# A hybrid decoder trunk on one core: norms spread by transposes, some norm sums from one operand, and first products, an attention turn and the last tile reordered

## The chip, the cores and the metric

The kernel runs on one core of a Trainium2 chip. The metric is the device time of one execution in microseconds. A kernel's time is the median of its runs; the profile is one further execution, with the time of every instruction on TensorE (matrix products into PSUM), VectorE, ScalarE, GpSimd and SyncE (which issues the DMAs).

## The reference, cut to what matters

Two residual layers over 1024 tokens of width 1024, all in float32, with a norm ahead of every mixer and feed-forward part and one at the end. Layer 0 mixes with gated DeltaNet heads and a short convolution, layer 1 with HGRN2 heads and dilated window attention in three patterns that are merged by their log-sum-exp.

```python
def rms_norm(x, g):
    xf = x.astype(jnp.float32)
    y = xf * lax.rsqrt(jnp.mean(xf * xf, axis=-1, keepdims=True) + EPS)
    return (y * g.astype(jnp.float32)).astype(x.dtype)
...
    for layer in range(DEPTH):
        i = layer // 2
        hn = rms_norm(h, norm_mix_g[layer])
        if layer % 2 == 0:
            h = h + mixer_ab(...)
        else:
            h = h + mixer_cd(...)
        hn = rms_norm(h, norm_ffn_g[layer])
        h = h + swiglu(hn, ffn_w_gate[layer], ffn_w_up[layer], ffn_w_down[layer])
    return rms_norm(h, norm_final_g)
...
    o_a = gated_delta_rule(q, k, v, g, beta)
    o_a = (rms_norm(o_a, norm_g) * jax.nn.silu(z...)).reshape(b, t, DN_VW)
...
    wts = jax.nn.softmax(jnp.stack(lses, axis=-1), axis=-1)
    o_d = jnp.einsum('bthpd,bthp->bthd', jnp.stack(outs, axis=3), wts)
```

## The kernel before, in words

Activations lie transposed: 128 features on the partitions, 512 tokens (a "half") along a row, eight such pieces a half. Every projection is a sum over eight pieces of three products each (`mm3`, lines 122 to 128): a float32 operand is split into a rounded high part and a rest (`split`: ScalarE makes the high part, VectorE the rest), and high x high, high x rest and rest x high are added in PSUM. So a projection of one 128-feature tile for one half is 24 products of 512 columns (`proj`). Weights come in tiles of 512 KB through two `raw` buffers, and are split into four `w` buffers (`wload`). PSUM has eight banks in three kinds: `psg` (2), `psu` (3), `psm` (3); a product that asks for a bank waits until the last reader of that bank's earlier tile is done.

The norms are made by the class `Trunk`. `piece` squares one of the eight pieces on ScalarE and adds it to `acc` (on GpSimd unless told otherwise), but keeps the last square apart (L183 to L187). `rms` (L189) sums over the features with one-column products against a column of 1/1024: four token blocks for `acc`, four for the last square (L199); a product of plain float32 operands runs as two instructions. VectorE adds EPS (L202) and GpSimd takes the power -0.5 (L204). `spread` (L208) brings the four columns of factors to a row on all partitions with four plain products of a broadcast column against the identity (L213). ScalarE and VectorE then scale.

The order of the work. Where `manual_schedule` names an engine, that engine's instructions run in the order in which they are written; elsewhere a planner orders them by costs and due times. Each engine's queue is run in order, SyncE's too. The places that matter here:

- The start (L2355 to L2397): by hand on TensorE, VectorE and ScalarE. The first four weight tiles are `w0` and `w1` twice (`coming` asks, `arrived` splits a whole tile); `scaled_in` makes the two parts of one piece of x, `squares` the squares with adds on VectorE. `mixer_ab` (L1140 to L1155) then makes three products of the first half, with the norm's sum and spread between, then a fourth, then two products of the second half around the second norm (`second(0)` to `second(3)`). `lead` takes such a product out of its bank on VectorE (L1137).
- `gated` (L1587 to L1608), once for each of eight chunks of the DeltaNet: a diagonal matrix is made of the norm factors on VectorE (L1600), and four plain products of head rows with it transpose and scale in one (L1603).
- `Up.turn` (L583 to L700), by hand: the start of each feed-forward part, and through `Pairs` of the layer-1 projections. `part_a` splits a weight; `early` holds for `Pairs`. `rms(1, between=low)` puts VectorE's small step (L202) where it is written.
- `mixer_cd`: value products, query and key products (`swa_qk`, which frees its bank at L1963), HGRN2 steps and attention steps are interleaved by `tick` and `run`. `turns` rotates the queries and keys of pattern 0 (three VectorE operations each, L1917 to L1919); `run` advances it with every second HGRN2 step. `combine` (L2141) merges three patterns' parts of one head and half: it loads the parts that lie in DRAM (L2149), waits one or two steps, computes on VectorE (L2157 to L2174) and transposes into a `psu` bank (L2181).
- `out_proj` (L1092): asks for the eight pieces of h of a half (`tr.begin`, L167) and then for the weights, pair by pair (L115); `save` writes h back (L217).
- `down` and, for its very last tile, `last` (L1014): the tile's 512 tokens as two halves of 256 columns with TensorE's order by hand, each followed by its norm, the scaling of all eight pieces (`scaled`, L2411) and the writing out.

Of the kernel before, what the change touches and what calls it, by code (L numbers as in the profile page):

```python
# [54 lines left out]
def hybrid_trunk_kernel(ctx: ExitStack, tc: tile.TileContext, x_t, w_all, w_down, w_ba, vecs, c_f, c_i, c_rope, out):  # L55
# [92 lines left out]
    class Trunk:  # L148
# [23 lines left out]
        def piece(self, half, d, eng=None, cols=ALL, n=None):  # L172
# [11 lines left out]
            if n == KT - 1:  # L184
                self.sq[half] = q
            else:
                (eng or G).tensor_tensor(a, a, q, op=ADD)  # L187

        def rms(self, half, cols=ALL, between=lambda: None):  # L189

            a = self.acc[half][:, cols]
            q = self.sq.pop(half)
# [4 lines left out]
            for i, x in enumerate((a, q)):  # L197
                for j in range(n):
                    T.matmul(st[:, j:j + 1], x[:, j * P:(j + 1) * P], onesn, start=i + j == 0, stop=i == 1,  # L199
                             skip_group_check=True)  # L200
# [7 lines left out]
        def spread(self, r):  # L208
# [3 lines left out]
            for j in range(n):  # L212
                T.matmul(pb[:, j * P:(j + 1) * P], r[:, j:j + 1].to_broadcast([P, P]), ident, start=True, stop=True)  # L213
# [39 lines left out]
    class Up:  # L253
# [335 lines left out]
        def turn(self, tr, row, b11, b21, hx, close, left, right):  # L589
# [21 lines left out]
            self.part_a(1, ga)  # L611
            self.part_a(2, w2)
# [5 lines left out]
            dg = tr.rms(1, between=low)  # L618
            self.p2(0, b21, psg())
# [364 lines left out]
    def down(layer, up, tr, hx, hr, src, step, after):  # L984
# [29 lines left out]
        def last(part, d):  # L1014

            a, b = slice(0, HT // 2), slice(HT // 2, HT)
            with tc.manual_schedule(engines={mybir.EngineType.PE}):
                oa, ob = psu(), psm()
                part(oa, range(NK), a)
                add(1, d, oa, a)  # L1020
                part(ob, range(3), b)
                r = tr.rms(1, a)
                part(ob, range(3, 7), b)
                scaled(1, a, tr.spread(r))
                part(ob, range(7, NK), b)
                add(1, d, ob, b)
                scaled(1, b, tr.spread(tr.rms(1, b)))
# [64 lines left out]
    def out_proj(name, cat_d, tr, src, order, half, hp, lead=None):  # L1092
# [18 lines left out]
    def mixer_ab(hn, rb, hp, tr, first, second, close):  # L1111
# [46 lines left out]
        with ExitStack() as es:  # L1158
# [305 lines left out]
            def delta(yd, xd, load_al, load_cx):  # L1464
# [123 lines left out]
                def gated(c):  # L1588
# [10 lines left out]
                    dg = bt("dgo", bufs=1)  # L1599
                    V.tensor_tensor(dg, ident[:, None, :].to_broadcast([P, 4, P]), hb(rr), op=MULT)  # L1600
# [55 lines left out]
    def mixer_cd(hn, hp, pairs):  # L1656
# [7 lines left out]
        with ExitStack() as es:  # L1664
# [320 lines left out]
            class Attend:  # L1985
# [114 lines left out]
                def outputs(self, n):  # L2100
# [8 lines left out]
                    if n % 2 == 0:  # L2109
                        return  # L2110
# [444 lines left out]
```

## Time and profile before

| what | us |
|---|---|
| three runs | 2591.68, 2594.03, 2596.03 |
| their median | 2594.03 |
| the profiled execution, whole | 2596.2 |
| its span, first to last instruction | 2594.4 |
| TensorE busy | 2557.3 |
| VectorE busy | 1666.6 |
| ScalarE busy | 1034.5 |
| GpSimd busy | 515.9 |

A row of the timeline is: start, duration, engine, line, operation, out<-in, shape, how many; in brackets the engine's idle time before it and what ended it. PE is TensorE's products, PEld its weight loads, DVE VectorE, ACT ScalarE, POOL GpSimd, SPq SyncE's issues. Matrix products are pipelined, so the time that one costs is from its start to the next one's start, not its duration. The mean clock granted to TensorE was 0.996 of full.

### The profile page before, as it was taken

The numbers are of one execution on the slowest core, as the hardware profiler recorded it, in microseconds if no ns is written. First come the engines' busy times: TensorE is split into PE (matmuls) and PEld (weight loads), VectorE is DVE, ScalarE is ACT, GpSimd is POOL, SyncE is SP. The second block draws the span as 40 slices with busy tenths as digits, with TensorE's granted clock in tenths as the row PEclk, the third lists the DMA queues.
The fourth block names the chain that finished last, engine by engine and source line by source line (L and its number), as shares of the span: only waits on it lengthen the run. The fifth ranks groups of instructions, "written<-read, shape, count | busy, mean of one in ns | idle before, by whom it ended". The sixth has DMA issues, their size and how long they took to land. (4 is left out here: it accounts for less than half of the span.)

```text
span 2594.4 us, 37707 instructions
## 1 busy us (share of the span) xinstructions
PE 2557.3 (99%) x14179; PEld 2131.5 (82%) x14179; DVE 1666.6 (64%) x2814; ACT 1034.5 (40%) x1855; POOL 515.9 (20%) x440
## 2 busy tenths in 40 slices
PE   8999999999999999999999999999999999999998
PEld 6888888888888888888888887888788888888887
DVE  7877776576655665557675576674667565566553
ACT  4432123343333345344344455564534333334442
POOL 1111021344333310023330000000023433331001
PEclk9999999999999999999999999999999999999999
DMA  4334446525556688643336676525652455668853
GB/s 143 124 113 135 136 132 204 182 66 174 171 196 209 203 288 300 188 132 130 118 114 229 200 225 212 147 87 179 212 195 73 171 177 195 203 210 281 280 177 119
DMA packets 286375, 456.03 MB, mean 176 GB/s; under 512 B 50128, under 2 KB 141040, under 8 KB 286064
## 3 DMA queue, kind: packets, MB, share of 16 engines
q1 hardware_dynamic: 286192, 453.62, 53.9%
q8 instruction: 111, 1.82, 0.3%
q14 instruction: 72, 0.59, 0.1%
HBM read 311.36 MB, written 142.16 MB: 175 GB/s over the span
## 5 line engine op out<-in xcount | busy, mean ns | idle before, releaser
L103 DVE TENSOR_TENSOR w<-raw,w 128x1024 fp32r<-128x1024 f32 (+1 forms) x319 | 384.1, 1207 | 134.7 <-ACT w L102 133.5
L102 ACT CAST w<-raw 128x1024 fp32r<-128x1024 f32 (+1 forms) x319 | 306.6, 963 | 274.1 <-PE psu L128 127.3
L126 PE MATMUL psu<-hnh,w 128*128 128x512 f32 x888 | 355.9, 401 | 10.5 <-ACT w L102 8.8
L128 PE MATMUL psu<-hnh,w 128*128 128x512 f32 x888 | 349.4, 394 | 0.2
L127 PE MATMUL psu<-hnl,w 128*128 128x512 f32 x888 | 348.5, 392 | 0.8 <-DVE hnl L2339 0.8
L126 PEld LDWEIGHTS psu<-hnh,w 128*128 128x128 f32 x888 | 168.3, 190 | 45.0 <-ACT w L102 8.9
L128 PEld LDWEIGHTS psu<-hnh,w 128*128 128x128 f32 x888 | 168.0, 189 | 36.9 <-DVE w L103 1.3
L127 PEld LDWEIGHTS psu<-hnl,w 128*128 128x128 f32 x888 | 168.3, 190 | 34.8 <-DVE hnl L2339 1.3
L187 POOL TENSOR_TENSOR acc<-acc,sq 128x512 f32<-128x512 f32 x48 | 70.5, 1469 | 524.5 <-ACT sq L183 410.6
L302 POOL TENSOR_TENSOR ws<-raw 128x512 f32<-128x512 f32 x50 | 72.8, 1455 | 424.4 <-DMA raw<-in_dram 330.5
L103 DVE TENSOR_TENSOR w<-ws,w 128x1024 fp32r<-128x1024 f32 x47 | 61.7, 1313 | 118.2 <-ACT w L102 118.2
L103 DVE TENSOR_TENSOR hidq<-hr,hidq 128x1024 fp32r<-128x1024 f32 x72 | 82.1, 1142 | 77.1 <-ACT hidq L102 76.9
L102 ACT CAST hidq<-hr 128x1024 fp32r<-128x1024 f32 x72 | 70.2, 979 | 103.2 <-DMA hr<-ts 59.5
L126 PE MATMUL psm<-hidq,w 128*128 128x512 f32 (+1 forms) x275 | 106.0, 385 | 0.0
L127 PE MATMUL psm<-hidq,w 128*128 128x512 f32 (+1 forms) x275 | 105.8, 385 | 0.0
L128 PE MATMUL psm<-hidq,w 128*128 128x512 f32 (+1 forms) x275 | 105.8, 385 | 0.0
L126 PE MATMUL psu<-t3h,w 128*128 128x512 f32 x224 | 87.3, 390 | 1.0 <-ACT u L365 1.0
L126 PE MATMUL psu<-t4h,w 128*128 128x512 f32 x224 | 87.5, 391 | 0.6 <-ACT c L372 0.5
L127 PE MATMUL psu<-t4l,w 128*128 128x512 f32 x224 | 87.2, 389 | 0.0
L127 PE MATMUL psu<-t3l,w 128*128 128x512 f32 x224 | 87.1, 389 | 0.0
L128 PE MATMUL psu<-t4h,w 128*128 128x512 f32 x224 | 87.1, 389 | 0.0
L128 PE MATMUL psu<-t3h,w 128*128 128x512 f32 x224 | 87.1, 389 | 0.0
(491 smaller groups left out, 6479.2 us busy)
## 6 DMA issues: line engine op xcount, KB each, us to landing
raw<-in_dram SPq DMA_DIRECT2D x227, 512.0 KB, 4.4
sd<-in_dram SPq DMA_DIRECT2D x44, 512.0 KB, 3.9
hid<-hid SPq DMA_DIRECT2D x88, 256.0 KB, 3.1
sd<-sd SPq DMA_DIRECT2D x44, 512.0 KB, 3.4
hr<-ts SPq DMA_DIRECT2D x40, 512.0 KB, 4.2
raw<-sd SPq DMA_DIRECT2D x40, 512.0 KB, 4.4
hd<-h SPq DMA_DIRECT2D x48, 256.0 KB, 3.8
h<-hd SPq DMA_DIRECT2D x48, 256.0 KB, 5.4
```

The lines of the kernel that those rows point to most:

```text
L102: S.copy(hi, src)
L103: eng.tensor_tensor(lo, src, hi.bitcast(F32), op=SUB)
L126: T.matmul(o, lh, rh, start=first and i == 0, stop=False, **kw)
L127: T.matmul(o, lh, rl, start=False, stop=False, **kw)
L128: T.matmul(o, ll, rh, start=False, stop=last and i == n - 1, **kw)
L187: (eng or G).tensor_tensor(a, a, q, op=ADD)
L302: G.tensor_tensor(s[:, HT:], b[:, :HT], b[:, HT:], op=ADD)
```

## The change

The norm: the last square is added like the others, except in second halves with GpSimd's adds; the sum takes one operand where there is one; the spread is four transposes.

```diff
             q = self.tmp("sq", bufs=2)[:, cols]
             S.activation(q, src, AF.Square)
-            if n == KT - 1:
+            if n == KT - 1 and half and eng is None:
                 self.sq[half] = q
...
-            q = self.sq.pop(half)
+            parts = [a, self.sq.pop(half)] if half in self.sq else [a]
...
-                T.matmul(pb[:, j * P:(j + 1) * P], r[:, j:j + 1].to_broadcast([P, P]), ident, start=True, stop=True)
+                T.transpose(pb[:, j * P:(j + 1) * P], r[:, j:j + 1].to_broadcast([P, P]), ident)
```

The mixer rows of layer 0 are scaled on VectorE and then transposed:

```diff
-                    V.tensor_tensor(dg, ident[:, None, :].to_broadcast([P, 4, P]), hb(rr), op=MULT)
+                    V.tensor_tensor(rows, os_all[c], hb(rr), op=MULT)
...
-                        T.matmul(o[:, h * P:(h + 1) * P], os_all[c][:, h, :], dg[:, h, :], start=True, stop=True)
+                        T.transpose(o[:, h * P:(h + 1) * P], rows[:, h, :], ident)
```

The start: sixteen products of constants into a bank that nothing reads; the first two weights split by halves, between the pieces of x; the first products by halves of their sum, and three of the second half ahead of the last `second`:

```diff
+    o = psg()
+    for _ in range(16):
+        T.matmul(o[:, 0:P], onesn.to_broadcast([P, P]), onesn.to_broadcast([P, P]), start=True, stop=True)
...
     scaled_in(0, 0)
-    first = [[arrived(*w0)], []]
+    first = [[w0[0], w1[0]], []]
+    for i in range(2):
+        arrived_half(i, *w0)
     for d in range(1, 4):
         scaled_in(0, d)
-    first[0].append(arrived(*w1))
+    for i in range(2):
+        arrived_half(i, *w1)
+        for d in range(4 + 2 * i, 6 + 2 * i):
+            scaled_in(0, d)
...
-        os3 = [proj(wk(wqk, 0), hn[0]), proj(wk(wqk, 1), hn[0])]
+        a, b = range(KH), range(KH, KT)
+        os3 = [proj(wk(wqk, i), hn[0], a, last=False) for i in range(2)]
+        for i in range(2):
+            proj(wk(wqk, i), hn[0], b, os3[i], first=False)
+        os3.append(proj(wk(wvz, 0), hn[0], a, last=False))
         r = tr.rms(0)
-        os3.append(proj(wk(wvz, 0), hn[0], range(KH), last=False))
+        proj(wk(wvz, 0), hn[0], b, os3[2], first=False)
+        o = proj(wk(wvz, 1), hn[0], a, psg(), last=False)
         pb = tr.spread(r)
-        proj(wk(wvz, 0), hn[0], range(KH, KT), os3[2], first=False)
+        early[0, 3] = proj(wk(wvz, 1), hn[0], b, o, first=False)
         second(0)
...
-        early[0, 3] = proj(wk(wvz, 1), hn[0])
         second(1)
         early[1, 0] = proj(wk(wqk, 0), hn[1])
+        early[1, 1] = proj(wk(wqk, 1), hn[1])
         second(2)
-        early[1, 1] = proj(wk(wqk, 1), hn[1])
+        early[1, 2] = proj(wk(wvz, 0), hn[1])
         second(3)
```

The turn of `Pairs`: two weight splits after the norm's small step.

```diff
             if not self.early:
                 self.part_a(0, g0)
-            self.part_a(1, ga)
-            self.part_a(2, w2)
+                self.part_a(1, ga)
+                self.part_a(2, w2)
...
             dg = tr.rms(1, between=low)
+            if self.early:
+                self.part_a(1, ga)
+                self.part_a(2, w2)
```

The output projection asks for h two pieces at a time:

```diff
-        tr.begin(half, src)
+        tr.begin(half, src, range(2))
         for d0 in range(0, KT, 2):
             w = ws.get(d0) or wload((name, d0), (name, d0 + 1))
+            if d0 + 2 < KT:
+                tr.load(half, src, range(d0 + 2, d0 + 4))
```

Layer 1's mixer: no rotation is advanced while query and key products are being made; the merge of a part that has just been computed asks for the two others one attention step earlier (`partners`, in the tile that the rotations used before, or in the old ones), and computes one step after its own part is there:

```diff
-                        if begun[0] % 2:
+                        if begun[0] % 2 and made[0] <= len(coming):
                             next(turner, None)
...
                     if n % 2 == 0:
+                        if self.p == 0 and (self.h, 1, 1) in ended:
+                            self.others = partners(self.h, n // 2)
                         return
...
-                    if p == 0 and (h, 1, 1) in ended:
-                        late.append(combine(h, g, (ol, sums)))
-                        next(late[-1])
+                    if self.others:
+                        late.append(combine(h, g, (ol, sums, *self.others)))
+                        self.others = None
                         return
...
                 yield
-                if unit or ahead:
+                if not own and (unit or ahead):
                     yield
```

The last tile: 256, 128 and 128 columns, by hand on VectorE and ScalarE too, each norm's spread later among the next part's products:

```diff
-            a, b = slice(0, HT // 2), slice(HT // 2, HT)
-            with tc.manual_schedule(engines={mybir.EngineType.PE}):
-                oa, ob = psu(), psm()
+            a, b, c = slice(0, HT // 2), slice(HT // 2, 3 * HT // 4), slice(3 * HT // 4, HT)
+            E = mybir.EngineType
+            with tc.manual_schedule(engines={E.PE, E.DVE, E.Activation}):
+                oa, ob, oc = (psu() for _ in range(3))
                 part(oa, range(NK), a)
                 add(1, d, oa, a)
-                part(ob, range(3), b)
-                r = tr.rms(1, a)
-                part(ob, range(3, 7), b)
-                scaled(1, a, tr.spread(r))
-                part(ob, range(7, NK), b)
+                part(ob, range(5), b)
+                ra = tr.rms(1, a)
+                part(ob, range(5, NK), b)
                 add(1, d, ob, b)
-                scaled(1, b, tr.spread(tr.rms(1, b)))
+                pa = tr.spread(ra)
+                scaled(1, a, pa)
+                part(oc, range(3), c)
+                rb = tr.rms(1, b)
+                part(oc, range(3, NK), c)
+                add(1, d, oc, c)
+                pb = tr.spread(rb)
+                rc = tr.rms(1, c)
+                scaled(1, b, pb)
+                scaled(1, c, tr.spread(rc))
```

More of the change, by code (lines that the diff above doesn't have):

```diff
@@ L196, in rms @@
             st = psm()
-            for i, x in enumerate((a, q)):
+            for i, x in enumerate(parts):
                 for j in range(n):
-                    T.matmul(st[:, j:j + 1], x[:, j * P:(j + 1) * P], onesn, start=i + j == 0, stop=i == 1,
-                             skip_group_check=True)
+                    T.matmul(st[:, j:j + 1], x[:, j * P:(j + 1) * P], onesn, start=i + j == 0,
+                             stop=i == len(parts) - 1, skip_group_check=True)
             v = self.tmp("v4", (4,), 2)[:, 0:n]
@@ L2139, in outputs, with outputs_of, partners @@
                         late.extend(combine(h, i) for i in range(2))
+            def outputs_of(h, g, p, a):
+                dma(a[:, :, 0:P + 2],
+                    scr_o[h, p, g * HT:(g + 1) * HT].rearrange("(j i) d -> i j d", i=P)[:, :, 0:P + 2])
+            def partners(h, g):
+                if g:
+                    both = tl("turn0", (2, 4, 132))
+                    ts = [both[:, p] for p in range(2)]
+                else:
+                    ts = [tl(f"cm{p}", (4, 132)) for p in range(2)]
+                for p, a in enumerate(ts):
+                    outputs_of(h, g, p, a)
+                return ts
             def combine(h, g, own=None):
@@ L2145, in combine @@
                         yield
-                t, st = ([own[0]], [own[1]]) if own else ([], [])
-                for p in range(2) if own else (2, 0, 1):
-                    a = tl(f"cm{p}", (4, 132))
-                    dma(a[:, :, 0:P + 2],
-                        scr_o[h, p, g * HT:(g + 1) * HT].rearrange("(j i) d -> i j d", i=P)[:, :, 0:P + 2])
-                    t.append(a)
-                    st.append(a[:, :, P:P + 2])
+                if own:
+                    t, st = [own[0], *own[2:]], [own[1]]
+                else:
+                    t, st = [tl("cm2", (4, 132))] + [tl(f"cm{p}", (4, 132)) for p in range(2)], []
+                    for p, a in zip((2, 0, 1), t):
+                        outputs_of(h, g, p, a)
+                st += [a[:, :, P:P + 2] for a in t[len(st):]]
                 yield
-                if unit or ahead:
+                if not own and (unit or ahead):
                     yield
@@ L2374, in hybrid_trunk_kernel, with arrived_half @@
     dma(cf[:, 0:P], c_f[:, 0:P])
+    o = psg()
+    for _ in range(16):
+        T.matmul(o[:, 0:P], onesn.to_broadcast([P, P]), onesn.to_broadcast([P, P]), start=True, stop=True)
+    def arrived_half(i, u, raw):
+        z = slice(i * HT, i * HT + HT)
+        split(u[:, 0, z], u[:, 1, z], raw[:, z])
     scaled_in(0, 0)
-    first = [[arrived(*w0)], []]
+    first = [[w0[0], w1[0]], []]
+    for i in range(2):
+        arrived_half(i, *w0)
     for d in range(1, 4):
         scaled_in(0, d)
-    first[0].append(arrived(*w1))
+    for i in range(2):
+        arrived_half(i, *w1)
+        for d in range(4 + 2 * i, 6 + 2 * i):
+            scaled_in(0, d)
     w0, w1 = coming(("ab", 8)), coming(("ab", 12))
@@ L2384, in hybrid_trunk_kernel @@
     dma(ci, c_i)
-    for d in range(4, KT):
-        scaled_in(0, d)
     squares(0, range(3))
```

6 lines of the change are left out of this document (3 added, 3 removed).

## The prediction

> **What bounds the kernel now.** I read the page first, then TensorE's waits, longest first, then the timeline around each of them.
>
> ```profile
> span 2594.4 us, 37707 instructions
> PE 2557.3 (99%) x14179; PEld 2131.5 (82%) x14179; DVE 1666.6 (64%) x2814; ACT 1034.5 (40%) x1855; POOL 515.9 (20%) x440
> ```
>
> The span is TensorE's: 99% busy. An edit can gain in three ways only: fewer or cheaper TensorE instructions, TensorE waits that go, and a clock that is not granted in full. The waits are few (us in all, times, longest):
>
> ```profile
> PE psu L126 <- ACT w L102: 8.8, 2, 6.9
> PE psu L126 <- DVE k L1963: 4.1, 1, 4.1
> PE psm L213 <- POOL r L204: 3.3, 2, 2.2
> PE psu L2181 <- DVE ol L2174: 2.1, 2, 1.6
> ```
>
> Of the first row 6.9 us is the start, so the other wait for a weight is 1.9. The clock is the third item. In the timeline (start, duration) a 512-column product follows its predecessor after 0.23 us, and after 0.42 us inside a stretch with half the clock. The table of windows (us, busy by engine, clock, DMA) shows such stretches, 3.41 us or twice that long:
>
> ```profile
> 24.54 0.40 PE L126 MATMUL psu<-hnh,w 128*128 128x512 f32 x1
> 24.77 0.39 PE L127 MATMUL psu<-hnl,w 128*128 128x512 f32 x1
> ...
> 26.19 0.63 PE L128 MATMUL psu<-hnh,w 128*128 128x512 f32 x1
> 26.61 0.63 PE L126 MATMUL psu<-hnh,w 128*128 128x512 f32 x1
> ```
>
> ```profile
> 25.09:28.50 3.41, 3.41 (x11) 2.76 (x10) 1.65 (x3) 0.00 (x0) 0.54 (x1) 0.50 0.25 97
> 1598.64:1602.05 3.41, 3.24 (x9) 2.59 (x10) 0.02 (x1) 0.00 (x0) 0.00 (x0) 0.50 0.98 309
> 1899.00:1905.83 6.83, 6.83 (x22) 5.67 (x22) 3.15 (x5) 2.82 (x3) 1.97 (x1) 0.50 0.79 246
> ```
>
> A stretch of 3.41 us at half clock costs 3.41 x (1 - 0.23/0.42) = 1.5 us. Each follows a wait or a run of one-column products.
>
> **The change part by part.** First the TensorE instructions (start of a block, then of what follows it; by line for the counts):
>
> ```profile
> 49.99 1.05 PE L213 MATMUL psm<-cf,r 128*128 128x128 f32 x8
> 50.80 0.48 PE L1183 MATMUL psu<-hnh,wba 128*16 128x512 f32 x1
> ```
>
> ```profile
> 1836.69 0.60 PE L2181 MATMUL psu<-cf,ol 128*128 128x128 f32 x4
> 1837.04 0.48 PE L126 MATMUL psu<-b22h,w 128*128 128x512 f32 x1
> ```
>
> ```profile
> 2557.89 1.03 PE L199 MATMUL psm<-onesn,sq 128*128 128x1 f32 x8
> 2558.78 0.49 PE L126 MATMUL psg<-hidq,w 128*128 128x512 f32 x1
> ```
>
> ```profile
> L213 PE MATMUL psm<-cf,r 128*128 128x128 f32 x80 | 11.2, 282 | 3.3 <-POOL r L204 3.3
> L1603 PE MATMUL psm<-dgo,os 128*128 128x128 f32 x64 | 8.5, 276 | 0.1
> ```
>
> Four plain products run as eight instructions, 0.81 us; four transposes of the same size as four, 0.35 us: 0.46 less. Spreads: x80 is nine whole ones and two half ones, 9 x 0.46 = 4.1 us (the halves are in the last tile, below). Mixer rows: x64 is eight chunks, 8 x 0.46 = 3.7 us; the VectorE multiply ahead of them keeps its size. Sums: the second operand's eight instructions take 0.89 us, and six norms lose them (first half of five, and the first mixer's second half): 5.3 us. Together 13.1 us. In their place one more add runs ahead of each of the six sums, on GpSimd or VectorE; more products lie between for all but the first and the one near 1896, where up to its length can be given back. [...]
>
> The start:
>
> ```profile
> 10.46 1.05 ACT L102 CAST w<-raw 128x1024 fp32r<-128x1024 f32 x1 [0.54 <-DMA raw<-in_dram]
> 20.40 1.48 DVE L187 TENSOR_TENSOR acc<-acc,sq 128x512 f32<-128x512 f32 x2
> 21.94 1.05 PE L199 MATMUL psm<-onesn,acc 128*128 128x1 f32 x8 [0.17 <-DVE acc L187]
> 52.41 1.28 DVE L1137 TENSOR_TENSOR xp<-psu,rb 128x512 f32<-128x512 f32 x2
> ```
>
> ```profile
> 30.00:60.00 30.00, 30.00 (x145) 21.96 (x143) 28.70 (x48) 13.54 (x22) 5.60 (x10) 1.00 0.14 45
> ```
>
> The 16 dummy products run while TensorE waits for data anyway; their 32 instructions, at 0.10 us or twice that at half clock, end between 4 and 7.5, when the first weight is there (6.9 before), so I cost them at nothing. The second weight lands at 10.4; its first half is cast by about 11.1, and 36 of the first 48 products then follow at 0.23: done near 19.5 instead of 21.9. With 12 more (22.2) the sum waits for VectorE, whose chain ended at 21.9 and now has another 0.74: 22.6. The low stretch there (0.17 idle and sixteen one-column instructions, 1.9 us) shrinks to 1.2, so I take the half-clock stretch at 25.09 as gone. Then three products for the second half are made ahead of the second spread, instead of two. They hold all three banks of their kind, and no other product can start until VectorE has read one (52.41 before; it is busy 28.70 of 30 us around it). By my count TensorE comes to that point at 49.7 and waits to about 52.1, with 24 products (5.5 us) more behind it than at 50.80 before: 4.1 us ahead, 2.7 of which are already counted (two spreads, two sums). That leaves 1.4. VectorE, so full here, will make TensorE wait for some of this later in the mixer: I take 1.0 back (bounds 0 and all 4.1). Net 0.4.
>
> The turn at 1164:
>
> ```profile
> 1163.39 1.22 DVE L103 TENSOR_TENSOR w<-raw,w 128x1024 fp32r<-128x1024 f32 x1
> 1166.74 1.16 PE L213 MATMUL psm<-cf,r 128*128 128x128 f32 x8 [2.21 <-POOL r L204]
> 1167.94 2.72 DVE L223 SCALAR_TENSOR_TENSOR h<-h,vec,psm 128x512 f32<-128x512 f32 x4 [2.13 <-PE psm L213]
> 1190.64 0.50 PE L128 MATMUL psg<-t1h,w 128*128 128x512 f32 x1 [0.48 <-DVE w L289]
> ```
>
> The norm's small VectorE step stands behind two weight splits of 1.22 us; they now come after it. The spread need not wait, but VectorE then has those splits ahead of its scaling, and sets the pace up to 1190: 1167.94 becomes about 1165.9. 2.0 us (bounds 1.0 and 2.4).
>
> The rotations in the attention products:
>
> ```profile
> 1592.35 0.69 DVE L1917 TENSOR_TENSOR rs<-rs,turn 128x512 f32<-128x512 f32 x1
> 1597.63 1.03 DVE L1963 TENSOR_TENSOR k<-psu,sw 128x512 f32<-128x512 f32 x1
> ```
>
> TensorE waits 4.1 us for the bank that L1963 frees. Behind it on VectorE stand the three operations of a rotation, 0.69 each; held back, they give 2.1 us and run under the next value products. Bounds: 0, and 4.1 with 1.5 for the half-clock stretch behind it. Value 2.1.
>
> Merging the attention parts, and the loads of the output projection:
>
> ```profile
> 1857.53 0.17 DVE L2158 TENSOR_TENSOR mx<-mx,cm 128x4 f32<-128x4 f32 x1 [1.93 <-DMA cm<-scr_o]
> ...
> 1886.20 2.44 SPq L167 DMA_DIRECT2D h<-hd  x5
> 1891.31 0.92 SPq L115 DMA_DIRECT2D raw<-in_dram  x2
> 1897.22 1.04 ACT L102 CAST w<-raw 128x1024 fp32r<-128x1024 f32 x1 [5.58 <-DMA raw<-in_dram]
> ```
>
> The parts are asked for one step of the attention earlier, so VectorE's waits for them go; with them TensorE's 2.1 us of L2181. The merge itself now starts a step later where nothing follows. The tiles that only change shape cost nothing: the rotations that used the shared one are done before. Value 2.0, bounds -1 and 3.5. In the projection eight loads of h stand in SP's queue and on the DMA engines ahead of the weight for which TensorE stops 1.9 us; now two do, the others follow weights. With that wait the two half-clock stretches go: 1.9 + 2 x 1.5 = 5.0 us (bounds 0 and 5.5). The later h loads have over 10 us to land.
>
> The last tile:
>
> ```profile
> 2577.32 0.28 PE L126 MATMUL psu<-hidq,w 128*128 128x256 f32 x1
> 2578.76 0.28 PE L126 MATMUL psm<-hidq,w 128*128 128x256 f32 x1
> ...
> 2584.05 0.50 PE L199 MATMUL psm<-onesn,acc 128*128 128x1 f32 x4
> 2588.12 2.42 DVE L2411 TENSOR_TENSOR h<-h,psm 128x1024 f32<-128x1024 f32 x3 [1.65 <-PE psm L213]
> ```
>
> Twelve products of 256 columns take 1.44 us, 0.12 each. Two quarters of 128 columns are 66 products in place of 33. No such product is in the trace. Nearest are the 128-column passes at 0.10 to 0.11, so 66 x 0.11 = 7.3 us in place of 4.0: 3.3 more. The other end is two passes for each, as a plain product of this width has: 0.22, another 7.3. Behind the last product stand 10.3 us now. A quarter needs about 1.5 us of scaling instead of 2.42, but with VectorE's order by hand the second quarter's 1.5 stands ahead of it: about 8.7. Net 1.7 us lost (bounds 0 and 9.0).
>
> **The sum.** 13.1 + 0.4 + 2.0 + 2.1 + 2.0 + 5.0 - 1.7 = 22.9 us. The profiled execution took 2596.2 us, 1.8 around its span; it becomes 2573.3. The median shown is 2594.0, 2.2 lower, so 2571.
>
> **The rivals.**
> - *Queues as before.* The loads and rotations are ordered by a planner outside the hand-written stretches; the weight at 1891.31 may stand behind a save of h as much as behind the loads (SP is in order), and the bank at 1594 may wait for another VectorE split. Then 2.1 + 2.0 + 5.0 = 9.1 us stay: 2580. For it: neither queue is written by hand there. Against it: six loads fewer stand in front.
> - *Two passes in the last tile.* 128-column products at 0.22: 2578. For it: plain products of this width have two passes. Against it: one instruction a product at 256 and 512.
> - *More goes than I count.* The clock stays full after 1594 as well, the banks come sooner, the last tile breaks even: about 2561.
> - *VectorE takes the cut.* TensorE's shorter blocks turn into waits for VectorE in the mixers, and the queues stay: 13.1 + 0.4 + 9.1 lost, 2594. Against it: outside the first 110 us VectorE has slack (64%).
> - *The clock gate shuts at the transposes* (slower). If they do not keep the clock up, each of the nine spreads and eight chunks costs a half-clock stretch: 17 x 1.5 = 26 us, 2597. [...] The transposes at 1836.69 stand outside every half-clock stretch, so the trace does not bear it out at this length.
>
> **How the numbers follow.** Forecast 2571 (2564 to 2577): 0.55. Queues as before 0.15, two passes 0.15, more goes 0.08, VectorE takes the cut 0.05, the gate shuts 0.02. The range 2561 to 2583 takes in the third rival's time and the first two's, with part of what lies beyond each, and leaves out the last two. This kernel's measurement can tell about 0.2% (5 us) from no change: faster 0.55 + 0.15 + 0.15 + 0.08 = 0.93, same 0.05, slower 0.02.
>
> **What would show it.** L213's and L1603's successors with blocks of 0.35 us; six sums of eight instructions; TensorE at full clock from about 6 us on and through 25 to 28; a wait of some 2 us at the first product after the second spread; no wait at the turn's spread; L1963's wait halved; no TensorE stop at the weight near 1896, and the clock full there; the last tile's 128-column step. I am wrong if the bank wait near 50 is over 5 us, if TensorE's waits between 60 and 110 grow by more than 2, or if that step is near 0.2.

## The result, and the profile after

| | before | after |
|---|---|---|
| median, us | 2594.31 (6 runs, 2591.68 to 2599.68) | 2574.34 (6 runs, 2570.22 to 2577.98) |
| profiled execution, whole | 2596.2 | 2570.22 |
| its span | 2594.4 | 2568.4 |

The ratio is 0.9922, 95% interval 0.9910 to 0.9934: 20.0 us less between the medians, where 22.9 were forecast, and 26.0 between the two profiled spans. The median lies inside the forecast's range of 2564 to 2577, 3.3 us above its 2571. The profiled execution of the changed kernel is the fastest of its six runs, that of the kernel before stands 1.9 us above its median; what makes one execution differ from the next is read further down.

From the page of the changed kernel (busy time, share and instructions by engine):

```profile
PE 2544.8 (99%) x14124; PEld 2120.3 (83%) x14124; DVE 1666.6 (65%) x2823; ACT 1034.8 (40%) x1859; POOL 522.6 (20%) x445
```

TensorE's busy time fell by 12.5 us, with 33 products added in the last tile and 32 instructions at the start. Its waits by what ended them (us in all, times, longest):

```profile
PE psu L126 <- ACT sw L1909: 2.4, 1, 2.4
PE psu L126 <- DVE k L1981: 2.1, 1, 2.1
...
PE psm L213 <- POOL r L204: 1.5, 2, 1.0
...
PE psm L199 <- POOL acc L187: 0.9, 1, 0.9
```

L1981 is the old L1963: 4.1 became 2.1. The waits for the merge (old L2181) and for the weight near 1896 are not in the list; a wait of a sum for GpSimd is new. The timeline has the new blocks, and the place where I expected a wait for a bank:

```profile
28.97 0.60 PE L213 MATMUL psm<-cf,r 128*128 128x128 f32 x4
29.33 0.48 PE L126 MATMUL psg<-hnh,w 128*128 128x512 f32 x1
...
43.04 0.95 PE L199 MATMUL psm<-onesn,acc 128*128 128x1 f32 x8
43.85 0.49 PE L126 MATMUL psu<-hnh,w 128*128 128x512 f32 x1
...
49.87 1.89 PE L1371 MATMUL psg<-kq 128*128 128x256 f32 x8
52.03 0.41 PE L1201 MATMUL psu<-hnh,wba 128*16 128x512 f32 x1 [0.27 <-DVE xp L1150]
...
338.87 0.60 PE L1621 MATMUL psm<-cf,dgo 128*128 128x128 f32 x4
339.23 0.48 PE L126 MATMUL psu<-hnh,w 128*128 128x512 f32 x1
```

From block to next start: spread 0.36 us, sum 0.81, mixer rows 0.36, as forecast. Where all three `psu` banks are held, the planner had put eight products into a `psg` bank (L1371), so TensorE stood still for only 0.27 us.

The table of windows (us, busy by engine, clock, DMA share, GB/s): full clock around 25 and 1899, and one half-clock stretch left ahead of TensorE's last product, behind the first wait of the list.

```profile
22.40:30.00 7.60, 7.53 (x39) 6.40 (x40) 3.12 (x8) 2.19 (x5) 1.47 (x1) 1.00 0.51 167
...
1840.00:1900.00 60.00, 58.95 (x266) 47.82 (x265) 33.84 (x42) 25.55 (x34) 14.23 (x10) 1.00 0.82 276
```

```profile
1546.64:1550.05 3.41, 1.34 (x11) 1.15 (x11) 2.41 (x8) 3.31 (x10) 0.00 (x0) 1.00 0.44 138
1550.05:1553.46 3.41, 3.12 (x7) 2.48 (x8) 1.88 (x5) 2.97 (x8) 0.00 (x0) 0.50 0.72 238
```

Where the 26.0 us came from is told by the lead: how much earlier the same piece of TensorE's work starts (a spread L213, a chunk's transposes, or the n-th product of lines 126 to 128).

| place (start before, after) | lead, us | gained since, of it cheaper instructions |
|---|---|---|
| first chunk's rows (345.04, 338.87) | 6.2 | 6.2, 2.7 |
| first feed-forward, second spread (529.16, 517.42) | 11.7 | 5.6, 5.0 |
| turn's spread (1166.74, 1151.89) | 14.9 | 3.1, 1.8 |
| end of the turn, product 4620 (1189.5, 1175.8) | 13.8 | -1.1, 0.5 |
| product 6720 (1720.0, 1703.6) | 16.4 | 2.6, 0 |
| behind the merge, product 7140 (1873.7, 1852.9) | 20.8 | 4.4, 0 |
| spread in the output projection (1918.95, 1892.89) | 26.1 | 5.3, 0.9 |
| last tile's first product (2574.81, 2547.88) | 26.9 | 0.9, 2.3 |
| end | 26.0 | -0.9, 0 |

### The profile page after: what moved, and what is told of

It is laid out like the page before. It is cut to its first block, busy times and chain, and to the rows that moved or that the text cites. A ratio compares the mean times of both kernels' runs of the same rounds, so it can differ in the third digit from the quotient of the medians.

```text
span 2568.4 us, 37628 instructions
## 1 busy us (share of the span) xinstructions
PE 2544.8 (99%) x14124; PEld 2120.3 (83%) x14124; DVE 1666.6 (65%) x2823; ACT 1034.8 (40%) x1859; POOL 522.6 (20%) x445
## 4 chain that ended last, share of the span: by engine, by line
PE 73%; DVE 6%; DMA 2%; ACT 1%; issue 1%; POOL 0%; SPq 0%; DVEq 0%; ACTq 0%; POOLq 0%
PE psu L126 13%; PE psu L128 13%; PE psu L127 13%; PE psg L126 5%; PE psg L128 5%; PE psg L127 5%; PE psm L128 4%; PE psm L127 4%; PE psm L126 4%; PE psm L2125 1%; DVE h L223 1%; DVE h L592 1%; PE psm L2067 1%; DMA raw<-in_dram 1%; DVE w L289 1%
## 5 line engine op out<-in xcount | busy, mean ns | idle before, releaser
L126 PE MATMUL psu<-hnh,w 128*128 128x512 f32 x880 | 350.9, 399 | 2.8 <-ACT sw L1909 2.4
L128 PE MATMUL psu<-hnh,w 128*128 128x512 f32 x880 | 345.1, 392 | 1.0 <-DVE w L103 1.0
L187 POOL TENSOR_TENSOR acc<-acc,sq 128x512 f32<-128x512 f32 x52 | 79.0, 1520 | 527.1 <-ACT sq L183 527.0
L126 PE MATMUL psm<-hidq,w 128*128 128x512 f32 x264 | 102.8, 389 | 0.0
L127 PE MATMUL psm<-hidq,w 128*128 128x512 f32 x264 | 102.8, 389 | 0.0
L128 PE MATMUL psm<-hidq,w 128*128 128x512 f32 x264 | 102.8, 389 | 0.0
L126 PE MATMUL psu<-hidq,w 128*128 128x512 f32 (+2 forms) x242 | 90.7, 375 | 0.0
L127 PE MATMUL psu<-hidq,w 128*128 128x512 f32 (+2 forms) x242 | 90.5, 374 | 0.0
L128 PE MATMUL psu<-hidq,w 128*128 128x512 f32 (+2 forms) x242 | 90.5, 374 | 0.0
L126 PE MATMUL psu<-t3h,w 128*128 128x512 f32 x224 | 87.3, 390 | 1.0 <-ACT u L365 1.0
L126 PE MATMUL psu<-t4h,w 128*128 128x512 f32 x224 | 87.5, 391 | 0.6 <-ACT c L372 0.6
L393 POOL TENSOR_TENSOR hid<-hid,c 128x512 f32<-128x512 f32 x44 | 61.7, 1402 | 125.8 <-ACT hid L392 103.4
```

Of the source, the lines that this page charges most:

```text
L126: T.matmul(o, lh, rh, start=first and i == 0, stop=False, **kw)
L127: T.matmul(o, lh, rl, start=False, stop=False, **kw)
L128: T.matmul(o, ll, rh, start=False, stop=last and i == n - 1, **kw)
L393: G.tensor_tensor(h, h, self.c22.pop(f), op=MULT)
```

## The experiments

Theories and rivals stand in each expectation. "Behind" and "lead" are counted from traces as in the table; product n is the n-th of TensorE's three-product lines, counted from 0. The changed kernel, run again beside three of the others, had 2573.15 us and a ratio of 0.9923 (0.9909 to 0.9937). The six versions of it that leave out one part (constants, order of the start, turn, rotations, merge, loads) have medians 3.5 to 6.0 us above that, also the constants and the turn, where the traces show no loss that lasts; the intervals overlap. So a median here does not price a part of 2 us, and the traces are read for it.

### Only the cheaper instructions

```diff
 (before.py)
-            if n == KT - 1:
+            if n == KT - 1 and half and eng is None:
...
-                T.matmul(pb[:, j * P:(j + 1) * P], r[:, j:j + 1].to_broadcast([P, P]), ident, start=True, stop=True)
+                T.transpose(pb[:, j * P:(j + 1) * P], r[:, j:j + 1].to_broadcast([P, P]), ident)
...
-                        T.matmul(o[:, h * P:(h + 1) * P], os_all[c][:, h, :], dg[:, h, :], start=True, stop=True)
+                        T.transpose(o[:, h * P:(h + 1) * P], rows[:, h, :], ident)
```

> The kernel before with only the cheaper instructions of the change: spreads and mixer rows as transposes, one-operand sums; every order as before. Theory (the cut lies on TensorE's path): 17 blocks of 0.35 us and six sums of 0.81 us, 13.1 us less, ratio about 0.995, TensorE 13 us ahead of the kernel before at its last tile, and the waits at the turn (2.2 us), at the bank of L1963 (4.1 us) and at the weight near 1896 (1.9 us) still there. Rival (VectorE takes the cut): less than 5 us ahead, with TensorE's waits for VectorE grown by 8 us or more.

2583.0 us, ratio 0.9963 (0.9950 to 0.9975); the span is 13.2 us shorter, and the last tile starts 12.7 us earlier. Its waits of TensorE are those of the kernel before:

```profile
PE psu L126 <- DVE k L1963: 4.1, 1, 4.1
PE psm L213 <- POOL r L204: 3.4, 2, 2.3
...
PE psm L199 <- DVE acc L187: 1.2, 2, 0.7
```

The cut lies on the path. The last row is its price: the first two sums now wait for one more add on VectorE. The medians give 10.5 us, with 6.5 to 13 inside the interval; the profile before, from which the trace's 13.2 is counted, stands about 2 us above its medians.

### The start: without the constants, in the old order, and alone

```diff
 (after.py)
-    for _ in range(16):
-        T.matmul(o[:, 0:P], onesn.to_broadcast([P, P]), onesn.to_broadcast([P, P]), start=True, stop=True)
```

> The changed kernel without its sixteen products of constants. My prediction priced them at nothing, for the time in which they run. Theory now (they open the clock): half clock until about 11 us, the first twenty products 0.42 us apart instead of 0.23, TensorE 1.5 to 2.5 us later than the changed kernel at product 60 and about as much at the end. Rival (TensorE waits for the operands there anyway, as at 7.75 and 9.88 us): within 0.5 us of the changed kernel from product 60 on.

2577.5 us, ratio 0.9939 (0.9925 to 0.9953). At product 60 TensorE is 0.2 us ahead of the changed kernel, at product 300 within 0.1: the rival holds. The first products do run at the step of half clock, 0.43 us apart from 6.9 to 7.7, but with the constants gone TensorE waits less for operands, and at 22 the sum waits for VectorE either way. What this execution lost, it lost far behind: 2.1 us at 351, where VectorE waited 3.3 us for a DMA (1.0 in the changed kernel), 2.0 us for a weight at 1911, and half-clock stretches at 351 and 1928.

```diff
 (after.py, mixer_ab)
-        os3 = [proj(wk(wqk, i), hn[0], a, last=False) for i in range(2)]
-        for i in range(2):
-            proj(wk(wqk, i), hn[0], b, os3[i], first=False)
-        os3.append(proj(wk(wvz, 0), hn[0], a, last=False))
+        os3 = [proj(wk(wqk, 0), hn[0]), proj(wk(wqk, 1), hn[0])]
         r = tr.rms(0)
...
-        early[1, 1] = proj(wk(wqk, 1), hn[1])
         second(2)
-        early[1, 2] = proj(wk(wvz, 0), hn[1])
+        early[1, 1] = proj(wk(wqk, 1), hn[1])
```

> The changed kernel with the first products in the order of before (whole sums one after the other, two of the second half ahead of the last step instead of three); weights still split by halves. Theory (the order fills the wait for a bank near 50 us and the first wait for operands): TensorE 1 to 2.5 us behind the changed kernel at product 300. Rival (VectorE sets the pace up to 110 us, whatever TensorE's order): within 0.5 us there, and the same time.

2576.68 us, ratio 0.9936 (0.9922 to 0.9951): 3.5 us above the changed kernel beside it. At product 300 TensorE is 6.9 us behind, more than either theory had. Its timeline and windows show why:

```profile
22.24 1.05 PE L199 MATMUL psm<-onesn,acc 128*128 128x1 f32 x8 [1.28 <-DVE acc L187]
...
43.00 1.05 PE L199 MATMUL psm<-onesn,acc 128*128 128x1 f32 x8 [1.20 <-DVE acc L187]
```

```profile
24.09:27.50 3.41, 3.41 (x10) 2.56 (x9) 2.19 (x5) 0.13 (x1) 0.95 (x1) 0.50 0.41 163
...
44.57:47.98 3.41, 3.41 (x10) 2.62 (x9) 3.41 (x6) 0.63 (x1) 1.16 (x1) 0.50 0.00 0
```

With the old order both one-operand sums come before VectorE's last add is done, and each wait brings a half-clock stretch of 1.5 us: 5.5 of the 6.9 us. They are not the worth of the new start. The run with only the cheaper instructions, whose start is the old one whole, is 2.8 us behind the changed kernel at product 300; the old order beside halved weights is worse than either start.

```diff
 (before.py: the new first products, constants and halved first weights, and nothing else)
+    for _ in range(16):
+        T.matmul(o[:, 0:P], onesn.to_broadcast([P, P]), onesn.to_broadcast([P, P]), start=True, stop=True)
...
+        os3 = [proj(wk(wqk, i), hn[0], a, last=False) for i in range(2)]
```

> The kernel before with only the new start: sixteen products of constants, first weights split by halves, the first products in the new order; plain spreads and sums of two operands. Theory (the order gains by itself): TensorE 3.0 to 3.9 us ahead of the kernel before at product 300 (6.2 us between the two traces there, 2.7 of them cheaper instructions), ratio about 0.9985. Rival (it is worth that only together with the one-operand sums, whose added step on VectorE makes the old order wait): less than 1.5 us ahead.

2591.97 us, ratio 0.9997 (0.9988 to 1.0005). In the trace TensorE is 3.1 us ahead at product 300, but 1.5 of it is the half-clock stretch at 25 that the one profiled execution of the kernel before had; the runs show no gain. The new start by itself is worth 0 to 3 us; beside one-operand sums its order keeps the two waits above away.

### The turn

```diff
 (after.py)
             if not self.early:
                 self.part_a(0, g0)
-                self.part_a(1, ga)
-                self.part_a(2, w2)
+            self.part_a(1, ga)
+            self.part_a(2, w2)
...
             dg = tr.rms(1, between=low)
-            if self.early:
-                self.part_a(1, ga)
-                self.part_a(2, w2)
```

> The changed kernel with the two weight splits of the turn at 1150 ahead of the norm's small step again. Theory (my term): the wait at the spread goes from 0.7 to about 2.3 us, TensorE 1.6 to 2.0 us behind the changed kernel at 1160, and still about 1 us behind at 1400, since the waits at 1163 and 1176 (1.3 and 0.7 us), where the moved splits now stand, shrink by 1. Rival (VectorE sets the pace of the turn whatever stands first): less than 0.3 us behind at 1400.

2576.71 us, ratio 0.9935 (0.9922 to 0.9948). TensorE is 1.6 us behind at product 4560 (1162) and level at 4620 (1176): the rival holds. First the undone kernel's timeline, then the changed kernel's:

```profile
1153.46 0.65 PE L213 MATMUL psm<-cf,r 128*128 128x128 f32 x4 [2.12 <-POOL r L204]
...
1154.14 2.73 DVE L223 SCALAR_TENSOR_TENSOR h<-h,vec,psm 128x512 f32<-128x512 f32 x4 [1.62 <-PE psm L213]
```

```profile
1152.02 2.31 DVE L103 TENSOR_TENSOR w<-raw,w 128x1024 fp32r<-128x1024 f32 x1
1154.25 2.71 DVE L223 SCALAR_TENSOR_TENSOR h<-h,vec,psm 128x512 f32<-128x512 f32 x4
...
1164.79 0.50 PE L127 MATMUL psm<-t1l,w 128*128 128x512 f32 x1 [1.10 <-DVE t1l L592]
```

The spread comes 1.6 us earlier, but the scaling starts at the same time, behind the moved splits. What TensorE gains at the spread it waits for at 1164.

VectorE's sum of work does not explain that: without the edit it stood idle for 1.62 us ahead of the scaling, with the edit not at all. Two things fill the gap. The row of splits begins 0.7 us later (1148.53, against 1147.83), since the load of `xa` ahead of it is waited for longer. And the last split takes 2.31 us, where the same one takes 1.22 without the edit, while GpSimd works beside it:

```profile
1151.82 1.43 POOL L592 TENSOR_TENSOR ws<-xa 128x512 f32<-128x512 f32 x1
```

That split takes 2.30 to 2.32 us in all ten traces that have the edit, and none of its row over 1.23 in the four that don't. That GpSimd is the cause was not tested. In the changed kernel's trace all 31 splits of 1024 columns that took over 1.8 us run beside a GpSimd instruction for 0.7 us or more; of the 384 that took 1.1 to 1.3 us, 50 do so for over 0.3 us.

### The rotations

```diff
 (after.py)
-                        if begun[0] % 2 and made[0] <= len(coming):
+                        if begun[0] % 2:
```

> The changed kernel with rotations advanced during the query and key products, as before. Theory (my term, three operations of 0.69 us ahead of L1981's add): its wait for the bank near 1582 goes from 2.25 to about 4.3 us, TensorE 2.1 us behind from there. Rival (a weight split of 1.22 us takes their place, in either order): the wait stays within 0.5 us of 2.25 and nothing is lost.

2577.5 us, ratio 0.9936 (0.9922 to 0.9949). The wait is 3.8 us in place of 2.1, with a half-clock stretch behind it. VectorE in this run:

```profile
1578.57 0.68 DVE L1936 TENSOR_TENSOR rs<-rs,turn 128x512 f32<-128x512 f32 x1
1579.17 1.21 DVE L103 TENSOR_TENSOR w<-raw,w 128x1024 fp32r<-128x1024 f32 x1
1580.31 0.68 DVE L1937 TENSOR_TENSOR rs<-rs 128x512 f32<-128x512 f32 x1
...
1582.11 1.21 DVE L103 TENSOR_TENSOR w<-raw,w 128x1024 fp32r<-128x1024 f32 x1
1583.24 1.02 DVE L1981 TENSOR_TENSOR k<-psu,sw 128x512 f32<-128x512 f32 x1
```

My theory holds, with 1.7 us in place of 2.1: the rotation's three operations stand ahead of L1981 again. The second weight split, 1.2 us, stands ahead of L1981's add in both kernels; its length is over half of the 2.1 us for which TensorE still waits.

### The merge

The four edits of the merge in `mixer_cd` undone: `partners` goes, and `combine` asks for both parts itself.

```diff
 (after.py)
-                        if self.p == 0 and (self.h, 1, 1) in ended:
-                            self.others = partners(self.h, n // 2)
...
-                    if self.others:
-                        late.append(combine(h, g, (ol, sums, *self.others)))
+                    if p == 0 and (h, 1, 1) in ended:
+                        late.append(combine(h, g, (ol, sums)))
+                        next(late[-1])
```

> The changed kernel with the merge of the attention parts as before (the two stored parts asked for when the third is done). Theory (the waits for those loads go): TensorE falls 2.0 us behind the changed kernel (my term) to 4.9 us (what the two traces show between 1766 and 1853), with VectorE's waits of about 2 us for the loaded parts and TensorE's 2.1 us of waits at the merge's transposes back. Rival (that stretch gained because the work came in another order): less than 1 us behind.

2577.21 us, ratio 0.9936 (0.9924 to 0.9948). From product 6720 to 7140 TensorE falls 4.5 us behind (from 1.95 to 6.46). Waits and timeline of this run:

```profile
PE psu L2199 <- DVE ol L2192: 2.3, 2, 1.7
...
PE psg L127 <- DVE hnl L103: 0.8, 2, 0.7
```

```profile
1833.25 0.17 DVE L2176 TENSOR_TENSOR mx<-mx,cm 128x4 f32<-128x4 f32 x1 [1.64 <-DMA cm<-scr_o]
1834.11 0.50 PE L127 MATMUL psg<-hnl,w 128*128 128x512 f32 x1 [0.67 <-DVE hnl L103]
...
1843.20 0.17 DVE L2176 TENSOR_TENSOR mx<-mx,cm 128x4 f32<-128x4 f32 x1 [2.08 <-DMA cm<-scr_o]
```

VectorE waits for the loaded part, and behind it in its queue stands the split of the output projection's operand (`hnl`), for which TensorE waits as well. Counted from start to start, so with the slower steps around each wait (0.34 us in place of 0.23 from 1837.13 on), the waits for `hnl` cost about 1.7 us, those at the transposes the rest.

### The loads of the output projection

```diff
 (after.py)
-        tr.begin(half, src, range(2))
+        tr.begin(half, src)
...
-            if d0 + 2 < KT:
-                tr.load(half, src, range(d0 + 2, d0 + 4))
```

> The changed kernel with the output projection asking for all eight pieces of h ahead of its weights, as before. Theory: the stop of about 1.9 us for a weight in the second half's projection comes back, with one or two half-clock stretches of 1.5 us behind it: 2 to 5 us later than the changed kernel from there on; the new wait of 1.05 us of the second norm's sum for GpSimd goes if the later loads of h are its cause. Rival (the weight waits for the saves of h): no stop, within 0.5 us of the changed kernel.

2579.18 us, ratio 0.9943 (0.9931 to 0.9955), the most that one part brought back. TensorE is 5.5 us behind at product 7320 and 4.1 at 7440, the second sum's wait being gone there, as expected. The longest wait is the sum's:

```profile
1877.96 1.87 PE L199 MATMUL psm<-onesn,acc 128*128 128x1 f32 x8 [2.91 <-POOL acc L187]
1880.15 0.80 PE L126 MATMUL psu<-hnh,w 128*128 128x512 f32 x1 [0.32 <-ACT w L102]
```

The planner put the sum at 1878, right behind the projection's last product, not at 1886.5 as in the changed kernel, and there it waits 2.9 us for the last square's add. For the weight TensorE then waits only 0.3 more. But the sum lies inside the stop for the weight, which comes 5.5 us later than in the changed kernel, as the product behind it does (1880.15, against 1874.71). Issues and the cast of that weight, in this run and then in the changed kernel:

```profile
1865.35 3.01 SPq L167 DMA_DIRECT2D h<-hd  x6
1870.37 0.32 SPq L217 DMA_DIRECT2D hd<-h  x1
...
1871.38 1.25 SPq L115 DMA_DIRECT2D raw<-in_dram  x2
...
1879.05 1.04 ACT L102 CAST w<-raw 128x1024 fp32r<-128x1024 f32 x1 [2.55 <-DMA raw<-in_dram]
```

```profile
1867.22 1.00 SPq L115 DMA_DIRECT2D raw<-in_dram  x2
...
1873.57 1.05 ACT L102 CAST w<-raw 128x1024 fp32r<-128x1024 f32 x1 [4.22 <-DMA raw<-in_dram]
```

So my theory holds. With the early loads the weight stands behind six of them in SyncE's queue, and behind a save of h that waits for VectorE until 1870.37; in the changed kernel it is asked ahead of that save. What the loads and the save cost each was not taken apart. The clock is half from 1877.0 to 1883.8.

### The last tile, and a faster version

```diff
 (after.py)
-            a, b, c = slice(0, HT // 2), slice(HT // 2, 3 * HT // 4), slice(3 * HT // 4, HT)
+            a, b = slice(0, HT // 2), slice(HT // 2, HT)
...
 (the order of before)
```

> The changed kernel with its last tile in two halves of 256 columns, as before. My term: 1.7 us faster; the two traces show 19.58 us from the tile's first product to the end before and 20.56 after, so 1.0 us. Theory besides (128-column products 0.11 us apart leave TensorE so little work that the clock may go to half among them, as it did from 2561.5 in the run without the hold): runs of this kernel have no half clock before the last product, their median is 1 to 4 us below the changed kernel's, and they spread less. Rival (the smaller end quarter pays for the slower products): within 0.5 us, in the trace too.

2572.71 us (2565.1 to 2574.06), ratio 0.9922 (0.9909 to 0.9936): the runs show no difference from the changed kernel. The trace has 19.08 us from the tile's first product to the end. The traces of all fourteen runs tell more:

| last tile | from its first product to the end, us |
|---|---|
| 256 and 256 (before, three runs with this order) | 19.58, 19.08, 19.08, 19.81 |
| 256, 128, 128, clock full to the last product | 20.55 or 20.56, five times |
| 256, 128, 128, clock half among the products | 25.00, 25.06, 25.41 |

The timeline of the changed kernel, then timeline and windows of the run without the hold:

```profile
2560.01 0.27 PE L126 MATMUL psu<-hidq,w 128*128 128x128 f32 x1
2560.12 0.27 PE L127 MATMUL psu<-hidq,w 128*128 128x128 f32 x1
```

```profile
2561.82 0.41 PE L127 MATMUL psu<-hidq,w 128*128 128x128 f32 x1
2562.03 0.41 PE L128 MATMUL psu<-hidq,w 128*128 128x128 f32 x1
```

```profile
2558.10:2561.51 3.41, 3.41 (x33) 3.41 (x33) 0.16 (x1) 0.92 (x2) 0.71 (x1) 1.00 0.00 0
2561.51:2564.93 3.42, 3.42 (x19) 3.42 (x18) 2.22 (x4) 0.71 (x2) 0.00 (x0) 0.50 0.02 5
```

The 128-column step is 0.11 us at full clock and 0.21 at half. So the tile loses 1.0 us to the kernel before in five of the eight profiled executions and 5.4 to 5.8 in three. Against the run with the old division and the same cheap instructions (19.08) it loses 1.5 and about 6.

```diff
 (after.py, the version with 384 and 128)
-                tr.piece(half, d0 + i)
+                tr.piece(half, d0 + i, V if half else None)
...
+            a, b = slice(0, 3 * HT // 4), slice(3 * HT // 4, HT)
...
+                pa = tr.spread(ra)
+                part(ob, range(8, NK), b)
+                scaled(1, a, pa, ((0, 4),))
+                add(1, d, ob, b)
+                scaled(1, a, pa, ((4, 6),))
+                rb = tr.rms(1, b)
+                scaled(1, a, pa, ((6, 8),))
+                scaled(1, b, tr.spread(rb))
```

> The changed kernel with two further edits: the second halves' norms add their squares on VectorE and sum one operand (the last one excepted), and the last tile goes as 384 and 128 columns. Theory: two sums of sixteen instructions become eight (0.89 us each), the wait of 1.05 us for GpSimd at the second one goes, and the last tile, 20.5 us from its first product to the end, takes 18.3 to 19.1 (33 products of 384 columns at an estimated 0.17 from the rows of 256 and 512, and 33 of 128 at 0.11): 4 to 5 us less than the changed kernel in all. Rival (VectorE's adds stand behind its weight splits): the sums wait as long as they got shorter, and only the tile's 1.4 to 2.2 us are gained.

2569.05 us (2568.13 to 2570.43), ratio 0.9903 (0.9889 to 0.9916), 4.1 us under the changed kernel beside it. The tile took 19.87 us, not 18.3 to 19.1: the clock was half from 2557.8 on. The two second-half sums are blocks of 0.91, but now wait 0.55 and 0.75 us for VectorE's add, so much of their gain went back, as the rival said.

```diff
 (the same, with two halves)
-            a, b = slice(0, 3 * HT // 4), slice(3 * HT // 4, HT)
+            a, b = slice(0, HT // 2), slice(HT // 2, HT)
```

> As the version with 384 and 128 columns in the last tile, but with two halves of 256, the second half's add put between the pieces of the first half's scaling. Theory: 19.1 us from the tile's first product to the end (19.58 before, less the 0.5 us that the add stood behind the scaling), no half clock before the last product in any execution; median 2568 to 2570, 1.5 us under the changed kernel for the tile and 1 to 3 us for the second halves' sums and the clock. Rival (384 and 128 is better, its last piece being the smaller): 0.5 us or more above it.

2565.44 us (2561.32 to 2568.83), ratio 0.9895 (0.9880 to 0.9910): faster than both kernels, 27.6 us under the one before, and 2.6 below the lower end of what I expected. The tile takes 18.72 us, at full clock to its last product. VectorE:

```profile
2555.56 0.42 DVE L1013 TENSOR_TENSOR h<-h,psu 128x256 f32<-128x256 f32 x1 [0.15 <-PE psu L128]
2555.90 0.68 DVE L2454 TENSOR_TENSOR h<-h,psm 128x512 f32<-128x512 f32 x1
```

The add of the second half no longer stands behind two of the scalings. Tile and earlier work together give 3.4 us in the trace (1.8 and 1.5); the rest of the 0.27% between this ratio and the changed kernel's was not traced. (The changed kernel's profiled execution is 4.1 us under its median, this one's 1.4 above.)

### The changed kernel again

> The changed kernel once more, on the chip and beside the runs of the kernel before that the other three share. Theory (what differs between executions of one kernel is where half-clock stretches fall): TensorE's waits over 0.3 us return at the same places with the same length within 0.3 us, while stretches of 3.41 us at half clock, 1.5 us each, stand at other places or in another number than the two of the first profile. Rival (loads vary): the waits themselves differ by 1 us or more.

2573.15 us (2570.98 to 2578.57). TensorE's waits return within 0.3 us, that of L1909 with 1.9 in place of 2.4 us excepted, but a wait of 1.1 us for a weight at 1910 is new. Half-clock stretches are at 1550 in both, and at 1929 in this one only. Both things differ between executions, so neither theory is whole. Every run's mean granted clock is on record, and it goes with the time: of the eleven runs of the changed kernel, the six at 0.998 or 0.999 took 2570.2 to 2573.2 us, the five at 0.995 to 0.997 took 2575.5 to 2578.6. Where the clock was lost in the runs without a profile is not known; the last tile at half clock would fit its 4.5 us.

## Why the prediction held, step by step

The direction, the forecast's own range and the two largest terms held; the smaller terms erred on both sides.

- **Cheaper instructions, 13.1 us.** Right block by block (0.36 and 0.81 us), and 12.7 to 13.2 us in the trace of that part alone; its runs give 10.5, with 13.1 just outside the interval, so some of it may go back into waits.
- **Start and banks, 0.4.** Mis-sized: 3.5 us (6.2 less 2.7) by the first chunk, 1.5 of it the half-clock stretch at 25 of the one profile before. The constants are worth nothing, as priced. The wait of 2.4 us for a bank was the failed step: other products fill it, 0.27 us is left. VectorE took little back later (6.2 us ahead at product 300 and at the first chunk).
- **The turn, 2.0.** Failed: nothing lasts beyond 1176. The working put the two splits ahead of the scaling, which is right, and took each at the 1.22 us of the profile before. In the new order one of them takes 2.31, and VectorE's row of splits begins 0.7 us later, so the scaling starts at 1154.25, against 1154.14 without the edit.
- **Rotations, 2.1.** Right: the wait went from 4.1 to 2.1, and by 1.7 us when this edit alone was undone. The half-clock stretch behind it is gone in both profiled executions of the changed kernel, but stands there in four versions of it (loads, merge and the two faster ones).
- **The merge, 2.0.** Mechanism right, mis-sized: 4.5 us. I priced TensorE's waits at the merge's own transposes and left out those for `hnl`, which stood behind the same wait on VectorE.
- **Loads of the projection, 5.0.** Right in size (5.5, then 4.1) and in cause: with early loads the weight comes 5.5 us later. The rival's save of h, which then stands ahead of the weight too, may be part of it. That a sum would be put into the stop was not foreseen, nor the new wait of 0.9 us for GpSimd at the second sum.
- **The last tile, -1.7.** One pass and a step of 0.11, as chosen; -1.0 at full clock (-1.5 against the old division with the same instructions). My rival of 0.22 a product came true by another road, the clock, in three of eight executions.

The terms add to 22.9 us; the traces have 26.0, the runs 20.0. Of the six between traces and runs, 1.9 are the kernel before's profile above its median and 4.1 the changed kernel's below its own; the latter goes with the clock, 0.998 in the profiled execution, down to 0.995 in the slower of its runs. That the sum came this near is partly luck: the start and the merge gave 3.1 and 2.5 us more than priced and made up for the turn's 2.0, and in five of the eleven executions, at a granted clock of 0.995 to 0.997, some of the surplus went back. The rivals: the queues did not stay as before; VectorE did not take the cut; no half-clock stretch follows the transposes, of which all 17 blocks ran at full clock.

## What to carry to other kernels

Where one engine sets the pace of a stretch, price a reordering by that engine's work up to the next result that the others need, and by what will run beside it in the new order: one moved split took 2.3 us there instead of 1.2, beside a GpSimd instruction of 1.43 us, which was not tested as the cause. The longest wait is not always the one that costs: a sum's wait of 2.9 us lay inside the stop for a weight. An operand dropped from a sum turns its work into an add on another engine; the gain of about 0.9 us was real only where the order left other products between, while with the old order two such sums waited 1.28 and 1.20 us for that add. Price a narrower last tile by the measured step, not by the width: it was 0.112 us at 128 columns, against 0.120 at 256.

## What the runs showed of the hardware

**The step of a product** of these weights was 0.227 us at 512 columns, 0.173 at 384 (the run with 384 and 128), 0.120 at 256 and 0.112 at 128, with one weight load for each product (PE and PEld x14124 each in the changed kernel): the last halving saved 0.008 us.

**The half-clock stretches of a trace lie on one grid.** Those of the changed kernel begin at 1550.05 and 2563.80, 297 times 3.4133 us apart; those of the kernel before at 25.09, 1598.64, 1899.01 and 2588.50, which are 461, 88 and 202 times that apart. The same wait brought such a stretch in one trace and none in another: the wait for L1981, 2.1 us in both, in windows of the grid, of the changed kernel and then of the run with the old merge:

```profile
1580.77:1584.18 3.41, 1.66 (x8) 1.04 (x6) 3.17 (x4) 1.26 (x2) 0.00 (x0) 1.00 0.39 138
1584.18:1587.60 3.42, 3.08 (x94) 2.59 (x96) 0.20 (x1) 0.97 (x2) 0.00 (x0) 1.00 0.43 153
```

```profile
1580.80:1584.21 3.41, 1.40 (x7) 0.82 (x5) 3.34 (x4) 1.02 (x1) 0.00 (x0) 1.00 0.36 141
1584.21:1587.62 3.41, 3.33 (x10) 2.67 (x10) 0.00 (x0) 0.00 (x0) 0.00 (x0) 0.50 0.45 154
```

With TensorE busy for 1.66 of 3.41 us the clock stayed full, with 1.40 it halved for the next window. So the same wait costs 2.1 us in one trace and, by the 1.5 us of a half-clock stretch, 3.6 in another. One-column products did not hold it at full: in the run with the old order the windows ahead of the half clock at 24.09 and 44.57 have 2.14 and 2.22 us of busy time, 0.9 of it a sum's. Without such sums, the clock stayed full behind windows with 1.66 us of TensorE's work (above) and 1.70 (1561.09 to 1564.51 in the kernel before), and went to half behind windows with 1.34 (1546.64 in the changed kernel), 1.40 (above) and 1.46 (1873.59 to 1877.00 in the run with the early loads). So in these windows 1.95 us without work, of 3.41, were enough, and 1.75 were not; that holds for them alone, and windows full of 128-column products, of which the next paragraph tells, are outside it.

**The clock halved among products of 128 columns while TensorE was never idle.** In the three executions with the last tile at half clock (without the hold, with the old turn, with the early loads), TensorE was busy for the whole 3.41 us of the window before it, which was full of 128-column products and held the whole of an eight-instruction sum; in the five others a window's edge cuts that sum or 256-column products share its window. That is a regularity in eight cases, not a tested cause. The run with 384 and 128 columns fits it: the window ahead of its half clock is full of 128-column products and most of a twelve-instruction sum.
